# The causal convolution of a recurrence: from VectorE adds to diagonal float32 products on TensorE

## The chip, the core and the metric

The kernel runs on one core of a Trainium2 chip. The metric is the time of one execution in device microseconds (us). TensorE does the matrix products into PSUM (the page writes PE for its matmuls and PEld for its weight loads), VectorE is DVE, ScalarE is ACT, GpSimd is POOL and SyncE is SP. Each engine works through its own list of instructions in order; where one waits, all behind it on that engine wait too.

## What is computed

One step of a hybrid encoder layer for 1024 frames of a new stream and 8 running streams of 16 frames (1152 columns in all). A projection feeds two groups, an RG-LRU recurrence and a sparse attention that keeps for each query the 256 best keys by an index score; an output projection and a feed-forward block follow. What the change touches is the convolution ahead of the recurrence:

```python
def causal_conv(xr, prev, w, b):
    T = xr.shape[1]
    xpad = jnp.concatenate([prev, xr], axis=1)     # prev: the 3 rows before
    y = b
    for j in range(CONV_W):                        # CONV_W = 4
        y = y + xpad[:, j:j + T] * w[j]            # w[j]: one factor per channel
    return y, xpad[:, -(CONV_W - 1):]
...
# rglru: xc -> gates r, i (block-diagonal products, sigmoid) -> a, b -> h_t = a_t * h_(t-1) + b_t
# dsa: vals, sel = top_k(idx_score, 256); attention over sel
```

## The kernel before

The program is written as generators ("streams") that a planner steps through: it keeps an estimate of the time at which each engine is free (`self.busy`, `self.pe`, lines 137 to 180) and lets the stream go on that is due first. So the order of the instructions on each engine comes out of those estimates, and after that a scheduler that works with the same priorities orders them again. Between the two, the order on an engine shifts when the estimated cost of anything shifts.

The stages, as the streams run: normalisation and keys (to about 80 us), index scores (to about 195 us), the recurrence (`lru`, 193 to 383 us by the trace), the query projection (`q_proj`), the first half of the output projection with the rotary embedding of the keys (`out_tile`, `k_rope`), attention (`attn`, `sample_attn`), the second half of the output projection, and the feed-forward block, which fills the time from about 770 us.

Two fillers run beside these stages: `topk` finds, bit by bit, the threshold of the 256th best score for each query. One group (tiles 2 to 4) counts on ACT, the other (tiles 5 to 8) on DVE: each of its 32 passes is four counts over 768, 896, 1024 and 528 columns and two or three very short instructions, first on the upper half of the float (`jk<-key,tk_cand`), then on the lower (`jk<-key,tk_cnt`). After the passes each tile gets its mask (`key<-jk`, `s<-s`, `jk<-key,tk_cnt,jk`). The fillers have a lower priority by 400 steps (`LATER`, line 153), so the planner puts a pass where it believes that DVE has nothing else to do. A pass waits for nothing but the pass before.

The recurrence has 4 chunks of 128 channels, each in a main stream (`lru_main`) and a gate stream (`lru_gate`, which is a projection and a GELU). The main stream goes over the 1152 columns in three thirds of 384. Each third is 24 products of the projection (`proj_T`, names `ps<-h,w`), then `conv(t, px)`: ACT copies the projection with its three columns of history into `xp`, ACT writes tap 3 and the bias into `xc`, and DVE adds taps 0, 1 and 2 (`xc<-xp,prm,xc`). In the last third the 8 running streams need adds of their own, so it has six in place of three. The result is split into a high and a low part (`xh`, ACT and POOL), and six products with the gates' block matrices follow (`ps<-xh,bd`). After all thirds: tanh, exp and sqrt on ACT, products on DVE, three scans on DVE (`tr<-tt,tr,ti`) and the copies of the last state (`tail<-tr`), with which a chunk ends. `xc`, `ti` and `tt` share 8 buffers (`LRU_C`); a chunk takes nine of them, so a chunk's second third waits for the scans of the chunk before. `lock("lru")` lets one main stream through its projection at a time.

`mm4` (line 207) is a product in plain float32; the compiler makes two instructions of each. Before, it is used only for a warm-up and for index scores of the running streams. All other products are of the `float32r` kind with operands split in two, three products for one (`mm3`).

Of the kernel before, what the change touches and what calls it, by code (L numbers as in the profile page):

```python
# [9 lines left out]
F32 = mybir.dt.float32  # L10
# [4 lines left out]
AF = mybir.ActivationFunctionType  # L15
# [15 lines left out]
NB = 8  # L31
# [50 lines left out]
class Kernel:  # L82
# [123 lines left out]

    def mm4(self, out, lhsT, rhs, start, stop):

        self.pe += 4 * rhs.shape[1] / 2400.0
        self.nc.tensor.matmul(out, lhsT, rhs, start=start, stop=stop)  # L210

    def tr(self, out, in_):
# [816 lines left out]
    def lru_main(self, n, c, lp):  # L1029
# [13 lines left out]
        bd = lp.tile([128, 2, 2, 128], F32R, tag="bd", name="bd", bufs=self.BD)  # L1043
        self.hi(bd[:, :, 0, :], braw, "pool")
        self.lo(bd[:, :, 1, :], braw, bd[:, :, 0, :], "pool")
        xps, xhs, xcs, G = [], [], [], []
        trs = []

# [2 lines left out]
                yield 0.3  # L1051
            self.c_free -= k

        def conv(t, px):
            self.begin()
            xc = third("xc")
            xcs.append(xc)
            n = 384 if t < 2 else 256
            xp = lp.tile([128, 411], F32, tag="xp", name="xp", bufs=self.XP)
            if t == 0:  # L1060
                nc.gpsimd.memset(xp[:, 0:3], 0.0)
            else:
                nc.gpsimd.tensor_scalar(xp[:, 0:3], xps[-1][:, 384:387], 1.0, 0.0, op0=ALU.mult, op1=ALU.add)
            S.activation(xp[:, 3:3 + n], px[:, :n], AF.Copy)
            xs = xp[:, 259:411].rearrange("p (b j) -> p b j", b=NB)
            if t == 2:
                S.activation(xs[:, :, 3:19], px[:, 256:384].rearrange("p (b j) -> p b j", b=NB), AF.Copy)
                nc.gpsimd.tensor_scalar(xs[:, :, 0:3], prm[:, c, 16:40].rearrange("p (b j) -> p b j", b=NB), 1.0, 0.0,
                                        op0=ALU.mult, op1=ALU.add)
            xps.append(xp)  # L1070
            S.activation(xc, px[:, :384], AF.Identity, scale=prm[:, c, 3:4], bias=prm[:, c, 4:5])
            for j in range(3):
                wj = prm[:, c, j:j + 1]
                o = xc[:, :n]
                V.scalar_tensor_tensor(o, xp[:, j:j + n], wj, o, op0=ALU.mult, op1=ALU.add)
                if t == 2:
                    o = xc[:, 256:384].rearrange("p (b j) -> p b j", b=NB)
                    V.scalar_tensor_tensor(o, xs[:, :, j:j + 16], wj, o, op0=ALU.mult, op1=ALU.add)
            if t == 2:
                nc.gpsimd.tensor_scalar(tail[:, c, 0:3], xp[:, 256:259], 1.0, 0.0, op0=ALU.mult, op1=ALU.add)  # L1080
                nc.gpsimd.tensor_scalar(tail[:, c, 3:27].rearrange("p (b j) -> p b j", b=NB), xs[:, :, 16:19], 1.0, 0.0,
                                        op0=ALU.mult, op1=ALU.add)
            xh = lp.tile([128, 2, 384], F32R, tag="xh", name="xh", bufs=self.XH)
            self.split(xh, xc, "act", "pool")
            xhs.append(xh)
            return self.end() + self.LRU_LAT
# [16 lines left out]
        for t in range(3):  # L1103
            px = self.ps()
            yield from self.proj_T(px[:, :384], w, self.h[t])
            yield from claim(1)
            ready.append(conv(t, px))
            yield 0.0
            yield from claim(2)
            while not t and not self.tr_free:  # L1110
                yield 0.3
            self.tr_free -= not t
            if t >= self.LAG:
                yield from self.until(ready[t - self.LAG])
                gates(t - self.LAG)
                yield 0.0
# [629 lines left out]
```

## Time and profile before

| | us |
|---|---|
| median of 3 runs | 1593.06 |
| lowest and highest of them | 1591.72, 1593.10 |
| the profiled execution, whole | 1592.46 |
| its span, first to last instruction | 1590.7 |

| engine | busy, us | share of the span |
|---|---|---|
| PE, matmuls | 1449.3 | 91% |
| PEld, weight loads | 1323.5 | 83% |
| DVE | 942.0 | 59% |
| ACT | 595.0 | 37% |
| POOL | 308.1 | 19% |

A busy PE is not PE at its peak: matmuls are pipelined and their ends are modelled, and TensorE's clock is granted in shares of full speed (1.00 is 2.4 GHz). The shares are averages over stages; the rows below tell them apart by stretches of the span.

### The profile page before, as it was taken

Reading aid. Unit: us, or ns where it says so; the run is one execution under the profiler, and the core shown is the slowest. Engines: PE = TensorE matmul, PEld = TensorE weight load, DVE = VectorE, ACT = ScalarE, POOL = GpSimd, SP = SyncE. Lnnn points to the kernel's source line nnn. Section 1 sums busy time; section 2 is a strip of 40 time slices with the busy share of each in tenths; the row PEclk is TensorE's granted clock in tenths of the full one; section 3 lists DMA queues with packets and bytes.
Section 4 is the critical chain, followed back from the end, with each engine's and each line's share of the span. In section 5 each row is a group of like instructions: output and inputs, shape, how many; then the busy total and the mean of one; then the engine's idle time right before and its main releaser. Section 6 shows DMA issues by size and latency. Waiting matters only on the chain.

```text
span 1590.7 us, 20862 instructions
## 1 busy us (share of the span) xinstructions
PE 1449.3 (91%) x7754; PEld 1323.5 (83%) x7754; DVE 942.0 (59%) x2024; ACT 595.0 (37%) x1417; POOL 308.1 (19%) x453
## 2 busy tenths in 40 slices
PE   6889887758856699999999999999999999999998
PEld 6877686758745588878999999999998989898987
DVE  7567899999999888858514242424333342424143
ACT  5458866764402687855411121202020202121100
POOL 4315135553675434500000000000000000000000
PEclk7999898888978799999999999999999999999999
DMA  7201101101400001220302020202020202011102
GB/s 237 54 16 42 34 16 29 29 27 34 152 30 22 1 2 39 66 68 25 96 14 59 22 66 14 76 4 80 0 80 1 80 10 71 27 54 42 38 1 119
DMA packets 93798, 74.65 MB, mean 47 GB/s; under 512 B 13236, under 2 KB 84532, under 8 KB 93696
## 3 DMA queue, kind: packets, MB, share of 16 engines
q1 hardware_dynamic: 93696, 73.32, 15.4%
q8 instruction: 61, 1.00, 0.3%
q14 instruction: 41, 0.34, 0.1%
HBM read 67.03 MB, written 6.27 MB: 46 GB/s over the span
## 4 chain that ended last, share of the span: by engine, by line
PE 67%; DVE 21%; issue 5%; ACT 4%; POOL 2%; DMA 1%; SPq 0%; DVEq 0%; ACTq 0%; POOLq 0%
PE ps L205 63%; DVE jk L66 8%; PE ps L215 3%; DVE xc L66 2%; DVE tk_cand L66 1%; DVE tr L66 1%; ACT jk L66 1%; DVE qn L66 1%; DVE s L66 1%; DVE ti L66 1%; ACT relu L66 1%; DMA x<-in_x_prompt_dram 1%; DVE acc L66 1%; ACT m L66 1%; DVE qeo L66 1%
## 5 line engine op out<-in xcount | busy, mean ns | idle before, releaser
L205 PE MATMUL ps<-hf,w 128*128 128x384 f32 x2556 | 460.5, 338 | 0.0
L205 PEld LDWEIGHTS ps<-hf,w 128*128 128x128 f32 x2556 | 451.4, 187 | 0.8
L205 PE MATMUL ps<-w,a 128*128 128x512 f32 x999 | 239.1, 390 | 0.0
L66 DVE TENSOR_TENSOR acc<-ps,acc 128x512 f32<-128x512 f32 x234 | 161.3, 690 | 119.2 <-PE ps L205 118.7
L205 PEld LDWEIGHTS ps<-w,a 128*128 128x128 f32 x999 | 187.3, 188 | 40.1
L66 DVE TENSOR_TENSOR sg<-ps,sg 128x384 f32<-128x384 f32 x66 | 36.8, 557 | 281.3 <-PE ps L205 280.8
L66 ACT ACTIVATE w<-raw 128x512 fp32r<-128x512 f32 x128 | 77.9, 629 | 300.1 <-PE ps L205 220.9
L66 DVE TENSOR_TENSOR w<-raw,w 128x512 fp32r<-128x512 f32 x116 | 76.8, 687 | 84.6 <-ACT w L66 84.4
L66 ACT ACTIVATE a<-sg 128x384 fp32r<-128x384 f32 x66 | 34.5, 523 | 221.8 <-DVE sg L66 221.8
L205 PE MATMUL ps<-hf,rest 128*128 128x384 f32 x612 | 114.5, 334 | 0.0
L205 PE MATMUL ps<-w,rest 128*128 128x512 f32 x324 | 85.2, 413 | 30.2 <-POOL rest L66 30.1
L205 PE MATMUL ps<-h,w 128*128 128x384 f32 x576 | 108.3, 348 | 0.0
L205 PEld LDWEIGHTS ps<-hf,rest 128*128 128x128 f32 x612 | 106.9, 188 | 0.2
L205 PEld LDWEIGHTS ps<-h,w 128*128 128x128 f32 x576 | 106.3, 197 | 0.0
L205 PEld LDWEIGHTS ps<-w,rest 128*128 128x128 f32 x324 | 62.0, 197 | 46.0 <-POOL rest L66 32.3
L205 PE MATMUL ps<-w,h 128*128 128x256 f32 (+1 forms) x600 | 98.3, 322 | 2.0 <-DVE to L66 2.0
L205 PEld LDWEIGHTS ps<-w,h 128*128 128x128 f32 x600 | 86.4, 197 | 8.3 <-DVE to L66 2.3
L66 ACT ACTIVATE jk<-s,tk_cand 128x384 bf16<-128x384 f32 (+2 forms) x96 | 69.7, 726 | 26.5 <-DVE tk_cand L66 24.1
L66 ACT ACTIVATE sg<-ps 128x384 f32<-128x384 f32 x66 | 32.1, 486 | 122.3 <-PE ps L205 122.3
L66 DVE TENSOR_SCALAR_CACHE_REDUCE jk<-key,tk_cnt 128x768 bf16<-128x768 int16 (+1 forms) x64 | 66.8, 1043 | 1.0
L66 DVE TENSOR_SCALAR_CACHE_REDUCE jk<-key,tk_cand 128x768 bf16<-128x768 bf16 (+1 forms) x64 | 66.7, 1041 | 0.2
L205 PE MATMUL ps<-xh,bd 128*128 128x384 f32 x72 | 22.2, 430 | 45.4 <-ACT xh L66 40.5
(263 smaller groups left out, 2179.4 us busy)
## 6 DMA issues: line engine op xcount, KB each, us to landing
raw<-in_w_ffn_in_dram SPq DMA_DIRECT2D x44, 512.0 KB
raw<-in_w_ffn_out_dram SPq DMA_DIRECT2D x22, 512.0 KB
raw<-in_w_in_dram SPq DMA_DIRECT2D x16, 512.0 KB
out_dram<-acc SPq DMA_DIRECT2D x9, 512.0 KB
x<-in_x_prompt_dram SPq DMA_DIRECT2D x8, 512.0 KB
acc<-in_x_prompt_dram SPq DMA_DIRECT2D x8, 512.0 KB
tab<-in_rope_dram SPq DMA_DIRECT2D x34, 64.0 KB
raw<-in_w_out_dram SPq DMA_DIRECT2D x4, 512.0 KB
```

The costliest lines, as they stand in the source:

```text
L66: return f(*args, **kw)
L205: self.nc.tensor.matmul(out, lhsT, rhs, start=start, stop=stop)
L215: self.nc.tensor.transpose(out, in_, self.ident[0:n, 0:n])
```

## The change

The adds on DVE go. `taps` is a new tile with four diagonal matrices for each chunk, made by four ACT instructions each from the identity (16 in all). `conv` is split in two: `streams(t, px)` makes the shifted input `xp` as before and the main stream now waits for it (by the planner's estimate) before it goes on; the new `conv(t)` multiplies the four shifted views of `xp` by the four diagonal matrices with `mm4`, summed in one PSUM bank (eight such products in the last third, four for 256 columns and four for 128), and ACT then writes `xc` from PSUM with the bias. `mm4`'s estimate counts all columns of a view with more than two dimensions.

```diff
     def mm4(self, out, lhsT, rhs, start, stop):
-        self.pe += 4 * rhs.shape[1] / 2400.0
+        self.pe += 4 * np.prod(rhs.shape[1:]) / 2400.0
...
+        taps = lp.tile([128, 4, 128], F32, tag="taps", name="taps", bufs=2)
+        for j in range(4):
+            S.activation(taps[:, j, :], self.ident, AF.Identity, scale=prm[:, c, j:j + 1])
...
-            S.activation(xc, px[:, :384], AF.Identity, scale=prm[:, c, 3:4], bias=prm[:, c, 4:5])
-            for j in range(3):
-                wj = prm[:, c, j:j + 1]
-                o = xc[:, :n]
-                V.scalar_tensor_tensor(o, xp[:, j:j + n], wj, o, op0=ALU.mult, op1=ALU.add)
-                if t == 2:
-                    o = xc[:, 256:384].rearrange("p (b j) -> p b j", b=NB)
-                    V.scalar_tensor_tensor(o, xs[:, :, j:j + 16], wj, o, op0=ALU.mult, op1=ALU.add)
...
+        def conv(t):
+            xp, n = xps[t], 384 if t < 2 else 256
+            pc = self.ps()
+            for j in range(4):
+                self.mm4(pc[:, :n], taps[:, j, :], xp[:, j:j + n], j == 0, j == 3)
+            if t == 2:
+                xs = xp[:, 259:411].rearrange("p (b j) -> p b j", b=NB)
+                for j in range(4):
+                    self.mm4(pc[:, 256:384].rearrange("p (b j) -> p b j", b=NB), taps[:, j, :], xs[:, :, j:j + 16],
+                             j == 0, j == 3)
+            S.activation(xc, pc[:, :384], AF.Identity, bias=prm[:, c, 4:5])
...
             yield from self.proj_T(px[:, :384], w, self.h[t])
+            yield from self.until(streams(t, px))
             yield from claim(1)
-            ready.append(conv(t, px))
+            ready.append(conv(t))
```

The order on the engines shifts with it. First PE at the first chunk's second third, before (`h` is the input, `w` the projection's weights, `xh,bd` the gates' products, `x12` counts equal rows):

```order
L205 MATMUL ps<-h_0_95,w 128x384 x12
L205 MATMUL ps<-h_1_96,w 128x384 x6
L205 MATMUL ps<-xh,bd 128x384 x2
L205 MATMUL ps<-h_0_99,w 128x384 x4
L205 MATMUL ps<-xh,bd 128x384 x4
L205 MATMUL ps<-h_0_99,w 128x384 x8
L205 MATMUL ps<-h_1_100,w 128x384 x12
L205 MATMUL ps<-xh,bd 128x384 x6
```

And now:

```order
L205 MATMUL ps<-h_0_95,w 128x384 x12
L205 MATMUL ps<-h_1_96,w 128x384 x11
L210 MATMUL ps<-xp,taps 128x384 x4
L205 MATMUL ps<-xh,bd 128x384 x6
L205 MATMUL ps<-h_0_99,w 128x384 x12
L205 MATMUL ps<-h_1_100,w 128x384 x12
L205 MATMUL ps<-h_1_96,w 128x384
L210 MATMUL ps<-xp,taps 128x256 x4
```

The products with `taps` stand between the projection of another stream and the gates' products of the third before.

Then DVE at the end of the last chunk, before (`jk,tk_cnt<-key,tk_cnt` is one count of a pass on the lower half, `tail<-tr` the copies that end the chunk):

```order
L66 SCALAR_TENSOR_TENSOR tr<-tt,ti 128x384
L66 TENSOR_SCALAR jk_911,tk_cnt<-key,tk_cnt 128x1024
L66 SCALAR_TENSOR_TENSOR tr<-tt,tr,ti 128x384
L66 TENSOR_SCALAR jk_911,tk_cnt<-key,tk_cnt 128x528
L66 SCALAR_TENSOR_TENSOR tr<-tt,tr,ti 128x384
L66 TENSOR_SCALAR tk_cand<-tk_cnt 128x4
L66 COPY tail<-tr 128x1
L66 COPY tail<-tr 128x8
L66 SCALAR_TENSOR_TENSOR tk_cnt<-tk_cand,tk_cnt 128x4
L66 TENSOR_SCALAR jk_911,tk_cnt<-key,tk_cnt 128x768
```

And now (`s_891` is the score of tile 5 and `s_890` that of tile 4, `key<-jk` the scan of a mask):

```order
L66 SCALAR_TENSOR_TENSOR tr<-tt,ti 128x384
L66 TENSOR_SCALAR jk_911<-s_891,tk_cnt 128x768
L66 SCALAR_TENSOR_TENSOR tr<-tt,tr,ti 128x384
L66 SCALAR_TENSOR_TENSOR key<-jk_911 128x768
L66 TENSOR_SCALAR s_891,tk_cnt<-s_891,tk_cnt 128x768
L66 TENSOR_SCALAR jk_912<-s_890,tk_cnt 128x640
L66 SCALAR_TENSOR_TENSOR tr<-tt,tr,ti 128x384
L66 TENSOR_SCALAR tk_cnt<-tk_cnt 128x1
L66 TENSOR_SCALAR s_890,tk_cnt<-s_890,tk_cnt 128x640
L66 COPY tail<-tr 128x1
L66 COPY tail<-tr 128x8
```

Before, 3 of the 16 passes on the lower half stand ahead of this place; now all 16 do, and the masks have begun.

Last, DVE at the first sums of the output projection (`acc<-ps,acc`), before:

```order
L66 TENSOR_SCALAR jk_911,tk_cnt<-key,tk_cnt 128x1024
L66 TENSOR_TENSOR qn<-qn,rp 128x256
L66 TENSOR_TENSOR tail<-tail 128x72
L66 TENSOR_TENSOR acc<-ps,acc 128x512
L66 TENSOR_TENSOR kn<-kn,tab 128x128
L66 TENSOR_TENSOR acc<-ps,acc 128x512
L66 TENSOR_SCALAR tk_cnt<-tk_cnt 128x1
L66 TENSOR_TENSOR qn<-qn,rp 128x256
L66 TENSOR_SCALAR jk_911,tk_cnt<-key,tk_cnt 128x528
```

And now (`qn` is the queries' rotary embedding, `kn` the keys'):

```order
L66 TENSOR_TENSOR kn<-kn,rp 128x128
L66 TENSOR_TENSOR acc<-ps,acc 128x512
L66 TENSOR_TENSOR qn<-qn,tab 128x256
L66 TENSOR_TENSOR acc<-ps,acc 128x512
L66 TENSOR_TENSOR qn<-qn,rp 128x256
L66 CAST jk_911<-s_894 128x528
L66 TENSOR_TENSOR qn<-qn,tab 128x256
L66 TENSOR_TENSOR qn<-qn,rp 128x256
```

Between the sums there are no counts left; the cast belongs to the sample attention's preparation, which runs when all masks are done.

## Rows read from the trace of the kernel before

**Rows 1.** The page: sums by engine, and three strips of 40 slices.

```profile
PE 1449.3 (91%) x7754; PEld 1323.5 (83%) x7754; DVE 942.0 (59%) x2024; ACT 595.0 (37%) x1417; POOL 308.1 (19%) x453
...
PE   6889887758856699999999999999999999999998
...
DVE  7567899999999888858514242424333342424143
...
PEclk7999898888978799999999999999999999999999
```

**Rows 2.** Stretches of the span: from:to, length, busy us, granted clock, DMA.

```profile
core 0: us, PE busy (x) PEld busy (x) DVE busy (x) ACT busy (x) POOL busy (x), PEclk, DMA share, GB/s
193.00:383.00 190.00, 142.30 (x783) 137.72 (x781) 187.28 (x470) 121.87 (x235) 81.46 (x111) 0.87 0.09 24
383.00:446.00 63.00, 50.15 (x334) 46.65 (x335) 62.28 (x137) 28.06 (x176) 39.73 (x64) 0.86 0.40 132
446.00:527.00 81.00, 49.55 (x195) 38.43 (x193) 79.15 (x158) 16.01 (x45) 46.28 (x61) 0.79 0.05 14
527.00:560.00 33.00, 26.40 (x132) 20.37 (x133) 29.02 (x108) 27.07 (x78) 19.21 (x31) 0.83 0.01 1
560.00:1590.00 1030.00, 1019.63 (x5501) 944.48 (x5499) 450.21 (x873) 277.71 (x569) 56.87 (x68) 1.00 0.15 45
```

**Rows 3.** Who waited for whom, 200 to 380: us in total, times, longest.

```profile
PE ps L205 <- ACT xh L66: 40.5, 8, 13.7
...
ACT xh L66 <- DVE xc L66: 11.9, 5, 3.9
```

**Rows 4.** Groups by form, 195 to 375: count | busy us, mean ns | idle before.

```profile
L66 DVE SCALAR_TENSOR_TENSOR xc<-xp,prm,xc 128x384 f32<-128x384 f32 x24 | 16.3, 681 | 0.0
...
L66 DVE SCALAR_TENSOR_TENSOR xc<-xp,prm,xc 128x256 f32<-128x256 f32 x12 | 8.1, 673 | 0.0
...
L66 DVE SCALAR_TENSOR_TENSOR xc<-xp,prm,xc 128x128 f32<-128x128 f32 x12 | 5.6, 464 | 0.0
...
L66 ACT ACTIVATE xp<-ps 128x128 f32<-128x128 f32 x4 | 1.1, 277 | 0.0
```

**Rows 5.** DVE in order of time: start us, us, what.

```profile
343.52 0.61 DVE L66 SCALAR_TENSOR_TENSOR xc<-xp,prm,xc 128x384 f32<-128x384 f32 x1
344.05 0.16 DVE L66 TENSOR_TENSOR ti<-ti,s 128x8 f32<-128x8 f32 x1
```

**Rows 6.** Float32 products of line 210: instruction groups, and six in order of time.

```profile
L210 PE MATMUL ps<-yF x32: 383/386/647, 122.3 to 185.4; 128*128 128x264 f32 x32
...
122.29 1.50 PE L210 MATMUL ps<-yF 128*128 128x264 f32 x6
```

**Rows 7.** Counts of the top-k on DVE, 380 to 440, as groups.

```profile
L66 DVE TENSOR_SCALAR_CACHE_REDUCE jk<-key,tk_cnt 128x528 bf16<-128x528 int16 (+3 forms) x35 | 36.3, 1037 | 0.6
```

**Rows 8.** DVE's three marks: last chunk's end, first sum, first attention score.

```profile
382.61 1.06 DVE L66 COPY tail<-tr 128x1 f32<-128x1 f32 x2
...
445.59 0.67 DVE L66 TENSOR_TENSOR acc<-ps,acc 128x512 f32<-128x512 f32 x1
...
526.67 0.29 DVE L66 CUSTOM_DVE_ANT_0 m<-ps,kn 128x128 f32<-128x128 f32 x1
```

**Rows 9.** 446 to 527: DVE and POOL work on tiles jk, and on tiles s.

```profile
446.00:527.00 81.00, 0.00 (x0) 32.56 (x48) 0.00 (x0) 6.18 (x4) 0.79 0.05 14
...
446.00:527.00 81.00, 7.63 (x12) 0.00 (x0) 9.64 (x8) 0.79 0.05 14
```

**Rows 10.** Who waited for whom, 440 to 500.

```profile
PE ps L205 <- POOL rest L66: 30.1, 5, 10.2
...
POOL kn L66 <- DVE kn L66: 11.3, 4, 5.6
```

**Rows 11.** PE in order of time: query projection and the first output tiles.

```profile
358.61 4.26 PE L205 MATMUL ps<-w,h 128*128 128x256 f32 x19
...
420.59 2.92 PE L205 MATMUL ps<-w,rest 128*128 128x512 f32 x12
...
426.12 2.93 PE L205 MATMUL ps<-w,rest 128*128 128x512 f32 x12
```

More of the change, by code (lines that the diff above doesn't have):

```diff
@@ L1052, in claim, with streams @@
             self.c_free -= k
-        def conv(t, px):
+        def streams(t, px):
             self.begin()
-            xc = third("xc")
-            xcs.append(xc)
             n = 384 if t < 2 else 256
@@ L1064, in conv @@
             S.activation(xp[:, 3:3 + n], px[:, :n], AF.Copy)
-            xs = xp[:, 259:411].rearrange("p (b j) -> p b j", b=NB)
             if t == 2:
+                xs = xp[:, 259:411].rearrange("p (b j) -> p b j", b=NB)
                 S.activation(xs[:, :, 3:19], px[:, 256:384].rearrange("p (b j) -> p b j", b=NB), AF.Copy)
@@ L1069, in conv @@
                                         op0=ALU.mult, op1=ALU.add)
-            xps.append(xp)
-            S.activation(xc, px[:, :384], AF.Identity, scale=prm[:, c, 3:4], bias=prm[:, c, 4:5])
-            for j in range(3):
-                wj = prm[:, c, j:j + 1]
-                o = xc[:, :n]
-                V.scalar_tensor_tensor(o, xp[:, j:j + n], wj, o, op0=ALU.mult, op1=ALU.add)
-                if t == 2:
-                    o = xc[:, 256:384].rearrange("p (b j) -> p b j", b=NB)
-                    V.scalar_tensor_tensor(o, xs[:, :, j:j + 16], wj, o, op0=ALU.mult, op1=ALU.add)
-            if t == 2:
                 nc.gpsimd.tensor_scalar(tail[:, c, 0:3], xp[:, 256:259], 1.0, 0.0, op0=ALU.mult, op1=ALU.add)
@@ L1082, in conv @@
                                         op0=ALU.mult, op1=ALU.add)
+            xps.append(xp)
+            return self.end()
+        def conv(t):
+            self.begin()
+            xp, n = xps[t], 384 if t < 2 else 256
[3 more added lines that the diff above has]
+            if t == 2:
+                xs = xp[:, 259:411].rearrange("p (b j) -> p b j", b=NB)
+                for j in range(4):
+                    self.mm4(pc[:, 256:384].rearrange("p (b j) -> p b j", b=NB), taps[:, j, :], xs[:, :, j:j + 16],
+                             j == 0, j == 3)
+            xc = third("xc")
+            xcs.append(xc)
+            S.activation(xc, pc[:, :384], AF.Identity, bias=prm[:, c, 4:5])
             xh = lp.tile([128, 2, 384], F32R, tag="xh", name="xh", bufs=self.XH)
```

## The prediction

> **What bounds the kernel now.** The first view is the page with its sums and strips [rows 1]. By the sums TensorE is the engine to spare: 1449.3 us of matmuls, 91% of the span, against 59% on DVE. The strips say that this is an average over two regimes. From about slice 21 PE is full and its clock granted in full; in slices 5 to 13 it is DVE that is full, and PE falls to 5 to 8 tenths at 0.7 to 0.9 of the clock.
>
> The second view, busy time by stretches, puts numbers to it [rows 2]. In the recurrence DVE is busy for 187.3 of 190 us, in the query projection for 62.3 of 63, in the output projection for 79.2 of 81: 328.7 of 334 us, 98%. PE has 142.3 of 190, 50.2 of 63 and 49.6 of 81. Only from 560 us on is PE the bound, with 1019.6 of 1030 us at clock 1.00. So the stretch from 193 to about 527 us lasts as long as DVE's list, and what comes after is a block of TensorE work that slides as a whole: a microsecond won at the first attention score, DVE's mark at 526.67 [rows 8], is one at the end.
>
> The third view, who waited for whom, agrees: in the recurrence PE waits 40.5 us for `xh`, and ACT waits for DVE's `xc` before it can write `xh` [rows 3].
>
> By the Trainium skill, Perfetto Trace Analysis, § Identifying the Most-Contended Engine, the engine with the highest occupancy is to be improved first, and for Tensor that occupancy is read as the busy share of its weight loads. Over the whole span that share is 83% against DVE's 59%; taken alone, the rule would have this change load the bound engine. Its neighbour section on optimization strategy allows that the contended engine changes over time, which is what [rows 2] show. What the first reading gives is a rival below.
>
> **Removed from DVE.** 24 adds of 384 columns, 12 of 256 and 12 of 128: 16.3 + 8.1 + 5.6 = 30.0 us busy [rows 4]. Instructions of DVE overlap a little: an add begins at 343.52 and lasts 0.61, and the next instruction begins at 344.05, 0.08 before its end [rows 5]. 48 x 0.08 = 4 us, so **26 us** of DVE's list go. Their bound from below is 24 (a step of 0.5 each), from above 30.
>
> **Added to TensorE.** Twelve thirds with four products of 384 columns (in the last thirds eight, of 256 and 128, together the same). Each is two instructions. The same line's float32 products in the trace: six instructions of 264 columns end 1.50 us after the first begins, the last being 0.386 long; five steps in 1.11 us, 0.222 each, 0.84 ns a column [rows 6]. So 384 columns take 0.32 us, and 12 x 4 x 2 x 0.32 = **31 us of PE**. Upper bound: 0.386 us each with no overlap for 264 columns, 0.56 for 384, 54 us. Both fit into the recurrence: 142.3 + 31 = 173 of 190 us [rows 2]; with 54 it would be 196, just over. I take 31, since the products with `taps` come in runs of eight as those of the row do in runs of six, and 142.3 is busy time that includes waiting for a slower clock.
>
> **Added elsewhere.** ACT writes 16 matrices at 0.28 us each [rows 4], 4.5 us, on an engine with 121.9 busy of 190 [rows 2]: nothing on the path. ACT's own `xc` stays, only its source is another PSUM bank. The chain of a third becomes ACT `xp`, PE 4 x 2 x 0.32 = 2.6 us, ACT `xc`, ACT `xh`; before, three adds at 0.53 to 0.68 with counts queued between them. About the same length, and DVE no longer in it. What hides it is the counts: they wait for nothing of this, so while there are passes left DVE has work whenever the chain is late. Without that cover the cost would be up to 2.6 us a third, 31 us.
>
> **Moved.** The planner sees DVE with more room and puts filler there: ahead of the last `tail<-tr`, at 382.6 [rows 8], stand now 13 more passes. 52 counts at 1.04 less the overlap, 1.00 [rows 7], 52 us; some 31 very short instructions at the 0.16 us of [rows 5], 5; eleven of the masks at 0.6 to 1 us [rows 9], 9; less 26. So DVE's list up to the end of the recurrence is **40 us longer**, and the recurrence would end near 423. This by itself is neither gain nor loss, since the filler had to be done anyway. It matters for what waits for the recurrence.
>
> The first sum of the output projection stands at 445.6 [rows 8]. Ahead of it now lies nearly all of the top-k work of the stretch 446 to 527: 48 instructions on `jk`, 32.6 us, those on `s`, 7.6 less some 3 that count in both [rows 9], a cast, and some 20 short ones, 3: 40 to 45. Nine adds of the queries' embedding, 5 us, go the other way. 42 - 5 - 26 makes +11, with the cast about +14: first sum near **460**. Ahead of the first score, at 526.7, the order has only six more mask instructions and three fewer others: -26 + 2 = -24, so **503** if DVE never waits.
>
> **What is late next.** Here lies the catch. The stage from first sum to first score was 81 us because DVE was full of counts. Without them DVE needs 79 - 42 + 5 = 42 us there. POOL needs 46.3 - 9.6 = 37 (its work on `s` is masks, gone ahead) [rows 2, 9]. PE needs seven output tiles of 5.53 us, the step between the first two [rows 11], 39. Three engines of 37 to 42 us wait for each other in turn: PE for POOL's `rest`, 30.1 us, POOL for DVE's `kn`, 11.3 [rows 10]. Those waits are long partly because DVE and POOL were then held up by masks and counts, and there is no cover left for them. The stage can't be under 42; if half of PE's 30 and all of the 11 stay in series with the shorter engines it is 39 + 15 + 11 = 65. I take 48 to 50, nearer the lower end, because the longest waits stood behind work that has left the stage. PE's own way there fits: its query projection begins at 358.6 [rows 11], in the gap behind the last chunk; 40 us more filler delays the scans that free the shared buffers, so I put that at about 385, and with 62 us to the first output tile (420.6 - 358.6), shorter where DVE was in its way, it comes near 447 to 457, just ahead of the first sum. First score then at 460 + 50 = **510**, 17 us earlier than 526.7.
>
> **The sum.** Profiled execution 1592.5 (span 1590.7 and 1.8 around it), less 17, 1575.5; the median of the runs is 0.6 above the profiled one: 1576, and I write **1575**.
>
> **The rivals.**
> First, the full gain: the output stage hides its chain and DVE's list stays the bound to the end of the stretch. 1592.5 - 26 = 1566 (1562 with the larger bound of the adds). For it: DVE was 98% busy in three stages with different chains [rows 2]. Against: 41 us of counts kept it so, and they stand earlier now.
> Second, the gain is eaten: the stage takes 61 to 68 us, the upper end above. 1589 to 1596, within what can be told from no change.
> Third, slower: the output stage was never as long as DVE's list but as its chain (POOL `kn` after DVE `kn`, `rest` after POOL, PE after `rest` [rows 10]) and keeps all its 81 us behind a first sum that comes 14 to 16 later. 1592.5 + 16 = 1608. It decides from the point where the stage shrinks by less than those 14 to 16 of 81. For it: PE's 30 us of waiting; against: DVE busy 79 of 81, and 40 of that leaves.
> Fourth, TensorE is the bound everywhere, as the whole span's shares have it [rows 1]: +31, 1623. Against: PE has 48 us to spare in the recurrence [rows 2]. The Trainium skill's rule named above, read on the whole span, is this rival.
> Fifth, DVE isn't relieved where it matters, because the planner returns all of it to filler and the recurrence ends 40 us later: that is what the order shows, and it is already in the sum; its harm would be the second or the third.
>
> **How the numbers follow.** Forecast (1568 to 1588): 0.55. Full gain (1560 to 1567): 0.17. Eaten: 0.13. Slower by the chain (1597 to 1610): 0.11. TensorE: 0.04. 0.2%, 3.2 us, is about what a measurement of this kernel tells from no change. Faster 0.55 + 0.17 = 0.72; same 0.13; slower 0.15. The range takes in the first three and leaves out the last two: 1560 to 1598.
>
> **What the profile after would show.** No `xc<-xp` on DVE; 128 instructions `ps<-xp,taps` on PE (4 x (4 + 4 + 8) x 2), 31 us in steps of 0.32 for 384 columns, else that term was wrong. DVE at 98% or more from 193 to about 420, the last tail copy near 423, the first sum near 460, the first score near 510, and the first idle time of DVE between those two, ended by POOL or PE. PE's wait for `xh` well under 40 us. If DVE idles for more than 5 us in the recurrence, the cover failed; if the stage from first sum to first score is above 65 us, the chain was the bound and the forecast is wrong; below 45, the full gain has it.

## The result

| | us |
|---|---|
| before, median | 1593.08 |
| after, median of 4 runs | 1607.45 |
| lowest and highest of them | 1604.22, 1608.10 |
| ratio after to before, 95% interval | 1.0087, 1.0070 to 1.0105 |
| the profiled execution of after, and its span | 1607.94, 1606.2 |

The changed kernel is slower by 14.4 us; 1575 was forecast, with a range of 1560 to 1598. The page of after, sums and the same three strips as in [rows 1]:

```profile
PE 1477.5 (92%) x7882; PEld 1341.0 (83%) x7882; DVE 929.6 (58%) x1976; ACT 593.4 (37%) x1430; POOL 307.9 (19%) x453
...
PE   6889878787487899999999999999999999999998
...
DVE  7557899999978788858624252424243333424243
...
PEclk9999999898698999999999999999999999999999
```

DVE lost 12.4 us of busy time where the adds were 30.0, and PE has a hole in slice 11 (about 402 to 442 us) that was not there. The same stretches as in [rows 2], cut at after's own marks (end of the recurrence, first sum, first score, 33 us more, the rest):

```profile
core 0: us, PE busy (x) PEld busy (x) DVE busy (x) ACT busy (x) POOL busy (x), PEclk, DMA share, GB/s
193.00:429.00 236.00, 176.45 (x931) 161.25 (x929) 229.51 (x569) 122.79 (x252) 81.22 (x115) 0.87 0.07 20
429.00:485.00 56.00, 46.47 (x310) 42.13 (x311) 44.88 (x65) 26.89 (x175) 52.44 (x60) 0.87 0.46 145
485.00:545.00 60.00, 47.83 (x200) 37.51 (x198) 45.09 (x86) 15.04 (x44) 40.39 (x65) 0.91 0.07 21
545.00:578.00 33.00, 29.09 (x159) 23.71 (x158) 28.96 (x112) 31.21 (x86) 14.54 (x29) 0.90 0.01 1
578.00:1606.00 1028.00, 1017.73 (x5484) 941.95 (x5482) 448.13 (x867) 274.57 (x562) 55.19 (x65) 1.00 0.15 45
```

The recurrence now takes 236 us instead of 190. The two stages behind it take 116 instead of 144, and there DVE idles for 26 of 116 us, where before it was busy for all but 2.6 of 144 [rows 2]. The marks of [rows 8], after, in order of time on DVE:

```profile
429.24 0.34 DVE L66 COPY tail<-tr 128x1 f32<-128x1 f32 x2
...
484.80 0.68 DVE L66 TENSOR_TENSOR acc<-ps,acc 128x512 f32<-128x512 f32 x1
...
545.13 0.29 DVE L66 CUSTOM_DVE_ANT_0 m<-ps,kn 128x128 f32<-128x128 f32 x1
...
722.63 0.68 DVE L66 TENSOR_TENSOR acc<-ps,acc 128x512 f32<-128x512 f32 x1
```

Against before, the recurrence ends 46.6 us later, the first sum comes 39.2 later, the first score 18.5. The last row is the first sum of the output projection's second half, and before it stands here:

```profile
706.97 0.68 DVE L66 TENSOR_TENSOR acc<-ps,acc 128x512 f32<-128x512 f32 x1
```

From this mark to the end of the span it is 883.7 us before and 883.5 after, and between 883.5 and 884.4 in every kernel of this study. So the whole question lies between 193 us and this mark.

**Where the 39 us at the first sum are from.** ScalarE (ACT) at the end of the last chunk, after, in order of time, with its wait in brackets:

```profile
392.49 1.35 ACT L66 ACTIVATE tr<-tr,m 128x1152 f32<-128x1152 f32 x1
415.43 1.28 ACT L66 ACT_TABLE_LOAD   x1 [21.59 <-DVE tr L66]
416.72 1.16 ACT L66 ACTIVATE tr<-tr 128x1152 f32<-128x1152 f32 x1
429.69 0.38 ACT L66 ACTIVATE qn<-ps 128x256 f32<-128x256 f32 x1 [11.81 <-DVE tail L66]
```

The exp (`tr<-tr,m`) is done at 393.8. The sqrt behind it needs DVE's `tr`, and its table load waits 21.6 us for it; before, and in gate11 below, where some of the filler is held back, the same wait is 5.8 and 3.3 us. Before:

```profile
372.57 1.28 ACT L66 ACT_TABLE_LOAD   x1 [5.84 <-DVE tr L66]
...
383.79 0.39 ACT L66 ACTIVATE qn<-ps 128x256 f32<-128x256 f32 x1 [8.75 <-DVE tk_cnt L66]
```

In gate11:

```profile
377.35 1.28 ACT L66 ACT_TABLE_LOAD   x1 [3.32 <-DVE tr L66]
...
388.60 0.39 ACT L66 ACTIVATE qn<-ps 128x256 f32<-128x256 f32 x1 [8.79 <-DVE tk_cand L66]
```

In after's 21.6 us DVE is not idle:

```profile
404.06 0.76 DVE L66 TENSOR_SCALAR_CACHE_REDUCE jk<-key,tk_cnt 128x528 bf16<-128x528 int16 x1
...
408.26 1.26 DVE L66 TENSOR_SCALAR_CACHE_REDUCE jk<-key,tk_cnt 128x1024 bf16<-128x1024 int16 x1
...
409.91 0.61 DVE L66 SCALAR_TENSOR_TENSOR jk<-ps,tk_cnt,jk 128x384 bf16<-128x384 f32 x1
...
411.12 2.05 DVE L66 SCALAR_TENSOR_TENSOR tt<-tr,tt 128x384 f32<-128x384 f32 x3
...
414.03 1.32 DVE L66 SCALAR_TENSOR_TENSOR tr<-tt 128x384 f32<-128x384 f32 x2
```

It counts: of the 17.3 us from 393.84 to 411.12 it is busy for 16.7, with 13.6 of them on `key`. The step `tt<-tr,tt`, whose inputs ACT had written by 393.8, starts at 411.12, behind passes that have that place in the list. From the end of the exp to the last tail copy it is 15.9 us before, 35.4 after and 13.9 in gate11.

The copies of the query projection out of PSUM (`qn<-ps`) wait for the tail copy itself. The first of them begins 0.1 us after the last tail copy ends, in after (429.58 and 429.69), before (383.67 and 383.79) and gate11 (388.49 and 388.60) alike, and so in every kernel of this study but hurry, where POOL's last read of a tile of the recurrence, `yF<-yF,tr`, comes 0.9 us later still and ends the wait. The program has a reason that fits all of them: the pool of `qn` is opened where the pool of the recurrence's tiles has been closed (lines 323 to 332), so that `qn` takes over their memory and has to wait until they have been read for the last time. Until then PE can run the projection ahead only as far as the eight PSUM banks (line 268) reach. It began at 384.62, had six tiles of 24 products by 404.0, and stood still for 24.0 us from there to the first output tile, against 5.0 us before and 5.8 in gate11:

```profile
384.62 4.47 PE L205 MATMUL ps<-w,h 128*128 128x256 f32 x24
...
389.68 14.29 PE L205 MATMUL ps<-w,h 128*128 128x256 f32 x120
410.58 0.82 PE L215 MATMUL ps<-ident,tail 128*36 128x128 f32 x3 [6.62 <-DVE jk L66]
420.20 4.43 PE L205 MATMUL ps<-w,h 128*128 128x256 f32 x24 [8.79 <-DVE jk L66]
429.63 0.40 PE L215 MATMUL ps<-ident,tail 128*36 128x128 f32 x1 [5.00 <-DVE tail L66]
433.60 32.81 PE L205 MATMUL ps<-w,h 128*128 128x256 f32 x264 [3.57 <-ACT sq L66]
466.25 2.91 PE L205 MATMUL ps<-w,rest 128*128 128x512 f32 x12
```

Its waits of 6.62 and 8.79 us end when a mask on DVE has read a bank (`jk<-ps,tk_cnt,jk`, to 410.52 above, and again to 420.14): the masks of tiles 2 to 4, which the order has moved ahead, use PSUM too, and so take two of the eight banks. In before and in gate11 their first scan stands behind the tail copy. The last two waits end with the tail copy and with ACT's copies behind it.

The rows for the same place before are [rows 11]: 62.0 us from the projection's begin to the first output tile, now 81.6, in gate11 60.4. From the last tail copy to the first output tile it is 37.9 us before and 36.9 after, and between 34 and 41 in every kernel here. So an end of the recurrence that comes 46.6 us later puts the first output tile off by nearly as much (45.7). The stages behind it win 30 of these back: the mark of the second half comes 15.7 us later.

### The profile page after: what moved, and what is told of

Its sections match the earlier page's. It is cut to its first block, busy times and chain, and to the rows that moved or that the text cites. A ratio compares the mean times of both kernels' runs of the same rounds, so it can differ in the third digit from the quotient of the medians.

```text
span 1606.2 us, 21084 instructions
## 1 busy us (share of the span) xinstructions
PE 1477.5 (92%) x7882; PEld 1341.0 (83%) x7882; DVE 929.6 (58%) x1976; ACT 593.4 (37%) x1430; POOL 307.9 (19%) x453
## 4 chain that ended last, share of the span: by engine, by line
PE 69%; DVE 16%; ACT 6%; POOL 4%; issue 4%; DMA 1%; SPq 0%; POOLq 0%; ACTq 0%; DVEq 0%
PE ps L205 65%; DVE jk L66 8%; PE ps L215 3%; DVE tr L66 1%; ACT jk L66 1%; DVE tk_cand L66 1%; POOL rp L66 1%; DVE s L66 1%; DVE ti L66 1%; ACT relu L66 1%; ACT m L66 1%; PE ps L210 1%; ACT qeo L66 1%; ACT yF L66 1%; POOL w L66 1%
## 5 line engine op out<-in xcount | busy, mean ns | idle before, releaser
L205 PE MATMUL ps<-w,h 128*128 128x256 f32 (+1 forms) x600 | 98.4, 323 | 12.4 <-DVE jk L66 8.8
L205 PEld LDWEIGHTS ps<-w,rest 128*128 128x128 f32 x324 | 61.8, 195 | 24.7 <-POOL rest L66 10.9
L210 PE MATMUL ps<-xp,taps 128*128 128x384 f32 (+2 forms) x128 | 39.7, 461 | 30.2 <-ACT xp L66 28.5
```

## The experiments

Two theories stood at first. **Order**: the filler that the planner and the scheduler put ahead of the recurrence's end does the harm. **Products**: the 31 us on PE do it, wherever the filler stands. The tool for both is a tiny DVE instruction (four columns) beside a pass's counts that reads a value of a chunk's `tr` and multiplies it by zero; the passes behind it can't be scheduled ahead of the instruction that wrote the value. In the gates this is the chunk's sqrt, which is written over the exp (the expectations call it the exp output); up to one pass still stands between it and the tail copies. "Counts ahead" are the instructions `jk,tk_cnt<-key` that stand in DVE's list ahead of the last `tail<-tr`, of 128 in all. Differences to the kernel before are to its runs on the same chip.

| kernel | counts ahead | last tail | first score | DVE idle, 193 to last tail | time, us | ratio, 95% interval |
|---|---|---|---|---|---|---|
| before | 76 | 382.7 | 526.7 | 2.7 | 1593.1 | |
| after | 128 | 429.3 | 545.1 | 6.5 | 1607.5 | 1.0070 to 1.0105 |
| hurry | 128 | 441.1 | 553.8 | 5.8 | 1615.4 | 1.0128 to 1.0158 |
| gate7 | 100 | 405.4 | 533.8 | 25.8 | 1594.9 | 1.0004 to 1.0023 |
| gate11 | 84 | 388.0 | 525.8 | 28.0 | 1588.9 | 0.9966 to 0.9985 |
| gate11_again | 84 | 388.8 | 526.9 | 27.2 | 1588.8 | 0.9972 to 0.9990 |
| gate13 | 76 | 388.2 | 526.3 | 29.2 | 1592.1 | 0.9984 to 1.0003 |
| noadds | 92 | 376.2 | 519.5 | 5.2 | 1579.0 | 0.9899 to 0.9929 |
| waits_alone | 92 | 383.9 | 515.4 | 5.7 | 1579.3 | 0.9897 to 0.9926 |
| gates_a | 94 | 404.5 | 542.1 | 24.7 | 1603.9 | 1.0054 to 1.0084 |
| gates_b | 102 | 402.3 | 537.7 | 18.1 | 1600.1 | 1.0031 to 1.0065 |
| no_dependency | 94 | 396.5 | 533.8 | 21.9 | 1598.8 | 1.0027 to 1.0051 |
| products_only | 74 | 391.8 | 535.6 | 16.3 | 1599.8 | 1.0022 to 1.0052 |
| one_tap | 104 | 393.2 | 523.9 | 4.1 | 1585.0 | 0.9936 to 0.9966 |
| short_chain | 94 | 391.6 | 530.3 | 11.3 | 1593.7 | 0.9998 to 1.0017 |
| before_held | 64 | 377.9 | 523.8 | 12.7 | 1600.7 | 1.0032 to 1.0062 |
| hybrid | 84 | 397.6 | 535.0 | 23.8 | 1599.1 | 1.0032 to 1.0063 |

### The order alone: hurry, gate7, gate11

**hurry**: the kernel before, with the order of after.

```diff
+        while self.pass_b > self.HURRY[c]:      # HURRY = (99, 13, 7, 0)
+            yield 0.3
         S.activation(trs[0], trs[0], AF.Exp, scale=m4[:, c:c + 1], bias=m4[:, c:c + 1])
+        if c:
+            x = trs[0][:, 0:4]
+            V.scalar_tensor_tensor(x, self.pass_t, 0.0, x, op0=ALU.mult, op1=ALU.add)
```

> The kernel before, with its adds on DVE and without products, but chunks 2, 3 and 4 may not begin their exp before 3, 9 and 16 lower-half passes stand ahead (a tiny DVE instruction reads the threshold of the pass): counts ahead of the chunks' tail copies 40, 83, 107, 128 instead of 40, 58, 64, 76; the changed kernel has 58, 76, 101, 128. The total work of DVE is the same. Theory 1: last tail at 382.6 + 52 = 435, and from there 116 us to the first score as in the changed kernel, 551 instead of 526.7: about 1615 us. Theory 2 or a view that filler is free wherever it stands: 1593.

1615.4, +22.9 us, the recurrence's end at 441.1 and 112.7 us from there to the first score. No work was changed but for three instructions of four columns: DVE did the same passes earlier, and then had 7 idle us between the recurrence's end and the first sum and 12 behind it. So filler ahead of the recurrence's end is not free. The order is not quite that of after: the second chunk has 83 counts ahead of its end where after has 76, and the recurrence ends 11.8 us later than there. The 22.9 us are the price of this order, not a part of after's 14.4.

**gate7, gate11**: the changed kernel, with one wait, ahead of lower-half pass 9 or 5.

```diff
+                if b == self.HOLD:              # 7 or 11
+                    while self.last_tr is None:
+                        yield 0.3
+                    nc.vector.scalar_tensor_tensor(t, self.last_tr, 0.0, t, op0=ALU.mult, op1=ALU.add)
                 yield from self.topk_count(g, t, True)
```

> The changed kernel with one more tiny DVE instruction: the lower-half pass number 9 (of 16) reads a value of the last chunk's exp output, so the seven passes from there and all masks can't stand ahead of it. Counts ahead of the last tail copy: 100 instead of 128 (76 before). Theory 1 (the harm is the filler that was pulled ahead of the recurrence's end; it holds back ScalarE's exp/sqrt chain and behind it the query projection, and leaves DVE nothing to do later): last tail copy at 382.6 + 24 - 26 = 381 instead of 429, DVE idle under 10 us between there and the first attention score, first score 505 to 515, 1570 to 1580 us. Theory 2 (the 31 us of float32 products on TensorE are the price, wherever the filler stands): the recurrence ends after 410 and the time stays above 1597.

> As the run before, but the wait stands at the fifth lower-half pass: 84 counts ahead of the last tail copy. Theory 1: DVE's own list would end the recurrence at 382.6 + 8 - 26 = 365; if the chain of ScalarE and TensorE allows that, DVE stays full and the first score again comes at 505 to 515, 1570 to 1580 us; if not, DVE idles in the recurrence for the difference, and the time is by so much worse than that of the wait at pass 9. Theory 2: above 1597.

1594.9 and 1588.9, +2.4 and -3.6: against after's +14.4 the order of a few passes is worth 12 and 18 us of the changed kernel, so its 1607 is not the price of the products alone. But neither came to 1570 to 1580, and DVE idled for 26 and 28 us inside the recurrence, which the first theory had only as a possibility for gate11. What bounds gate11 there is seen in the last chunks, up to the last product with the gates' matrices (`ps<-xh,bd`, done at 370.0) and from there to the recurrence's end, beside the whole recurrence:

```profile
193.00:388.00 195.00, 168.40 (x913) 155.28 (x911) 167.00 (x439) 120.80 (x248) 76.77 (x111) 0.93 0.09 24
330.00:370.00 40.00, 39.46 (x224) 36.26 (x223) 22.16 (x49) 19.68 (x33) 27.12 (x35) 1.00 0.14 40
370.00:388.00 18.00, 15.90 (x136) 15.68 (x134) 12.09 (x25) 6.45 (x7) 4.78 (x8) 1.00 0.01 2
```

From 330 to 370 us PE is busy for 39.5 of 40 us at a granted clock of 1.00, all but 3.5 of it on products of the recurrence, and DVE for 22. With little filler in the way PE sets when the last chunk's products are done. The 18 us behind them are the chain through ACT and DVE, as before (18.6, from 364.1); PE is busy there too, but with the query projection, which does not end the recurrence.

### What the removal is worth: noadds, waits_alone

**noadds** is the kernel before without the loop over taps 0 to 2:

```diff
-            for j in range(3):
...
-                V.scalar_tensor_tensor(o, xp[:, j:j + n], wj, o, op0=ALU.mult, op1=ALU.add)
...
-                    V.scalar_tensor_tensor(o, xs[:, :, j:j + 16], wj, o, op0=ALU.mult, op1=ALU.add)
```

> The kernel before with taps 0 to 2 left out: 48 adds on DVE gone, no products on TensorE, nothing else edited (the output lacks these taps). 92 counts ahead of the last tail copy, 16 more than before. What the removal is worth at most. Theory 1: tail at 382.6 + 16 - 26 = 373, DVE's list shorter by 26 at the first score, 1567 to 1575 us. Theory 2: the same, since no products are there. Theory 3 (what DVE is relieved of is lost to waits anyway, whatever the order): 1585 or more.

1579.0, 13.5 us less than before, between the forecasts of the first and the third theory: half of the 26. From 193 us to the mark of the second half the time in which DVE runs anything (covered time) fell from 470.9 to 448.4, 22.5, and its idle time grew from 43.0 to 51.0, 8. **waits_alone** adds the four waits of gates_a to it:

> The run without adds and without products (taps 0 to 2 left out of the output), now with the four waits of the run with waits a. Counts ahead of the tail copies 44, 64, 76, 92, as without the waits; so it shows what the waits themselves cost. If they are free: tail 376 to 379, 1577 to 1582 us, and the difference to waits a, some 25 us, is the price of the products. If they cost 5 to 10 us of DVE's idle time: tail 382 to 386, 1584 to 1590, and the products cost 14 to 20.

1579.3: the tail comes 7.7 us later and the first sum 8.7, the time is the same. The waits are free here, and neither mark is a measure of the time by itself.

### What the products cost: gates_a, gates_b, no_dependency, products_only

**gates_a** is the changed kernel with counts ahead as in noadds, by four waits:

```diff
+    HOLD = {10: 0, 15: 1, 18: 2, 22: 3}         # pass: chunk
...
+        self.nc.vector.scalar_tensor_tensor(cnt, self.last_tr[c], 0.0, cnt, op0=ALU.mult, op1=ALU.add)
```

> The changed kernel with four tiny DVE instructions that make passes 11, 16, 19 and 23 of 32 read a value of the exp output of chunks 1, 2, 3 and 4. Counts ahead of the chunks' tail copies: 46, 64, 76, 94, almost as without the adds (44, 64, 76, 92; 1579 us) and with the changed kernel's 58, 76, 101, 128 undone. So against the run without adds this shows the price of the products alone, and against the changed kernel that of the order alone. Theory 1 (products fit beside DVE, 31 us of PE into 48 us of room): last tail 376 to 380, 1579 to 1585 us. Rival (with the filler spread as before, TensorE is the recurrence's bound, as in the wait at pass 5, where it was busy 55 of 58 us in the last two chunks): DVE idles some 10 to 25 us in the recurrence, tail near 385 to 390, 1587 to 1593.

> As the run before with the waits one to two passes later (passes 12, 17, 21 and 25): 50, 68, 86, 102 counts ahead of the tail copies, eight more at the end, 8 us of DVE. Where DVE's list ends the recurrence, tail and time come up to 8 us later than there, less what DVE idled; where TensorE ends it, the time is the same and DVE's idle time shorter.

1603.9, 24.6 us over waits_alone with the same waits and nearly the same counts, and worse than the rival's 1587 to 1593. gates_b, eight counts more, ends the recurrence at 402.3 instead of 404.5 with 7 us less idle time on DVE, and is 3.9 us faster, which neither branch of its expectation had: it was not DVE's list that ended it. In **no_dependency** the products multiply the diagonal matrices by themselves, so nothing waits for anything new:

```diff
-                self.mm4(pc[:, :n], taps[:, j, :], xp[:, j:j + n], j == 0, j == 3)
+                self.mm4(pc[:, :384], taps[:, j, :], taps[:, 0:3, :], j == 0, j == 3)
...
-            S.activation(xc, pc[:, :384], AF.Identity, bias=prm[:, c, 4:5])
+            S.activation(xc, px[:, :384], AF.Identity, scale=prm[:, c, 3:4], bias=prm[:, c, 4:5])
```

> The run with waits a, with all products, but on constant operands (the diagonal matrices by themselves), so that TensorE waits for nothing and nobody waits for them; xc is written as in the run without adds (taps 0 to 2 left out of the output). Counts ahead of the tail copies 46, 64, 76, 94. Theory C (what is paid is TensorE's time itself, because its idle time in the recurrence is no room but part of the chain): tail and time as with waits a, 400 or later, about 1600. Theory D (TensorE has room, only the dependency costs): tail at 376 to 382, 1579 to 1585.

1598.8: 19.5 of the 24.6 us are there although nothing waits for the products. The place where they come in is PE's chain: its last product with the gates' matrices is done at 355.2 in waits_alone, at 369.7 here and at 382.8 in gates_a. What else no_dependency keeps of the change, a PSUM bank for each third, the 16 matrices on ACT and the wait for `xp` in the planner's order, was not taken away by itself. **products_only** puts the same constant products into the kernel before, adds kept:

> The kernel before, its adds on DVE kept, with the twelve sets of four float32 products (31 us of TensorE) put in on constant operands, whose result nobody reads, and waits that hold the filler where it was: counts ahead of the tail copies 46, 58, 62, 74 (before: 40, 58, 64, 76). My step that 31 us fit into TensorE's 48 idle us of the recurrence: tail at 383 to 386, 1593 to 1596 us. Theory C (that idle time is no room: TensorE waits there for a chain that goes through it, and each us of products lengthens it): tail 395 to 405, DVE idle 12 us or more there, 1603 to 1612.

1599.8, +6.4 us: between the two forecasts. The recurrence, 193 to 392 us:

```profile
193.00:392.00 199.00, 173.55 (x878) 155.70 (x877) 182.65 (x471) 129.45 (x256) 80.03 (x111) 0.93 0.08 23
```

PE went from 142.3 [rows 2] to 173.6 us busy: that is the 31. The stage grew by 9 all the same, with PE's idle time down from 47 to 25 and DVE's up from 3 to 16. So some two thirds of the products went into PE's idle time, and the rest made the stage longer. That PE's remaining idle time is waiting for a chain that runs through it fits, but is not shown by itself; and the waits that hold the filler may have a price of their own here, as they have in before_held below.

### Length or hop: one_tap, short_chain, hybrid

**one_tap** keeps one of the four products (`range(1)`), without waits; **short_chain** the same with the waits of gates_a.

> The changed kernel with one of the four products for each third (the output lacks taps 1 to 3; TensorE has 8 us of them instead of 31), no waits added: the scheduler itself then puts 52, 64, 84, 104 counts ahead of the tail copies. Theory: what pulls filler ahead is how long the scheduler holds the products, and the time follows the counts: near the run with waits b, 1583 to 1592, well below 1607.

> The run with waits a, with one product for each third in place of four (taps 1 to 3 left out of the output): the same counts ahead of the tail copies (46, 64, 76, 94), the same place in the chain (TensorE waits for xp, ScalarE for TensorE), 8 us of products instead of 31. There the last tail came at 404.5, and at 376.2 without products. Theory A (the length of the products sits on the recurrence's chain): tail at 376 + 28 x 8 / 31 = 383, 1583 to 1587 us. Theory B (it is the extra hop, TensorE's in-order list waiting for ScalarE's xp, whatever the products' length): tail near 400, about 1600 us.

one_tap: 1585.0, as expected, 22 us below after. With a quarter of the products the scheduler pulled 28 counts ahead of the place they had before, instead of 52, and DVE stayed filled (4.1 us idle). short_chain: 1593.7, between the two theories. Its work is that of one_tap; the waits, free without products, cost some 8 us here. So their length is a part of the products' price, and not in proportion: 8 us of them with their hop cost 14 over waits_alone, 31 cost 25. And a price found with the waits holds for the order that the waits make: without them the same 8 us cost 6 (one_tap over noadds).

**hybrid** is gate11 with tap 0 back on DVE, 8 us less on PE:

```diff
-            for j in range(4):
...
+            for j in range(1, 4):
...
+            V.scalar_tensor_tensor(o, xp[:, 0:n], prm[:, c, 0:1], o, op0=ALU.mult, op1=ALU.add)
...
```

> The changed kernel with the wait at pass 5 (run gate11: 1588.9 us, DVE idle 28 us in the recurrence, TensorE idle only 24), and tap 0 given back to DVE: three products for each third, then one add. TensorE has 8 us less, DVE 9 us more, which its idle time there should take. If TensorE's time is what ends the recurrence, tail near 382 and 1582 to 1586 us. If the add in the chain (ScalarE xc, DVE add, ScalarE xh) waits behind counts again: 1589 to 1596.

1599.1, 10 us worse than gate11 and above both forecasts. The waits in its recurrence, us in total, times, longest:

```profile
PE ps L205 <- ACT xh L66: 21.0, 4, 6.5
...
ACT xh L66 <- DVE xc L66: 15.6, 6, 8.8
```

These are the two of [rows 3], which the change had all but taken away (PE's wait for `xh` is 4.8 us in gate11). One DVE step in the chain brings them back, behind whatever DVE has in its list. So gate11 is not only bound by the length of PE's work; that the chain no longer passes through DVE also lets PE run through. The counts differ a little (54 and 68 ahead of the first two chunks' ends, in gate11 58 and 76).

### From the other side: before_held, gate13, gate11_again

**before_held** is the kernel before with waits at two passes (`HOLD = {13: 1, 14: 2}`), 12 counts fewer ahead.

> The kernel before with two waits of the kind used above (passes 14 and 15 read the exp of chunks 2 and 3): 40, 57, 62, 64 counts ahead of the tail copies instead of 40, 58, 64, 76. Its adds stay on DVE. If the filler in the last chunk costs about its own time, as the run with more filler ahead had it (+52 counts, +58 us of tail, +22 us of time), 12 counts fewer bring the tail 8 to 12 us earlier and the time down by 3 to 6, to 1587 to 1590. If DVE's list is the bound from 193 to 527 us as I read it in the prediction, the time can't fall: 1593 or a little more.

1600.7, +7.4, above both forecasts, though the recurrence ends 4.8 us earlier and the first score comes 2.8 earlier. The last mask's count on DVE moved from 533.5 to 553.0, and the masks are read by the attention: the mark of the second half comes 7.0 later (714.0). That the late masks put it off is read from the order; no run moved them alone. It would mean that the filler has a due time on both sides. This also corrects a step of the prediction: the first score is not yet the place from which all slides as a block.

> As the run with the wait at pass 5 of the lower half, two passes earlier: 58, 72, 72, 76 counts ahead of the tail copies, in sum the 76 of the kernel before. Best version so far if the trend of the waits at passes 9 and 5 goes on (1594.9, 1588.9): 1584 to 1588, tail near 382. If DVE's idle time now costs as much as the earlier tail brings: 1588 to 1592.

> The kernel of run gate11 once more, with more rounds: the interval there was 0.9966 to 0.9985 of the kernel before. If that holds: 1587 to 1590 us beside 1592 to 1594.

gate13 gives 1592.1, not told apart from before, where the trend forecast 1584 to 1588: fewer counts ahead than in gate11 gain nothing. gate11_again gives 1588.8, ratio 0.9981 (0.9972 to 0.9990): the one order in which the change is a gain, by 3 us, shown twice.

## Why the prediction was wrong

**Where the error lies.** The first score was put at 510 and came at 545.1, 35 us later. 6 of them were there at the recurrence's end (423 forecast, 429.3 measured), 19 more were added on the way to the first sum (37 us forecast, 55.5 measured), and 10 in the stage behind it (50 and 60.3).

**The bound** was half right. DVE is busy for 98% of 193 to 527 us, but a good part of it is filler that is put wherever DVE would idle, so a full DVE doesn't show that its list sets the end. Taking 26 us off the list gave 13.5 (noadds). The Trainium skill, Perfetto Trace Analysis, § Identifying the Most-Contended Engine, calls occupancy "a fair measure of how close you are to roofline" for Vector. It does not say what a microsecond off that engine is worth, and here it was worth half. (PE is full from slice 15 of the strips on, not from "about slice 21"; [rows 2] have it right, at 560 us.)

**Removed, 26 us**: the size held. Covered time fell by 22.5 in noadds. The step from there to the time didn't.

**Added, 31 us**: the size held where PE did not wait ahead of the products: PE's busy time went from 142.3 to 173.6 in products_only, and eight instructions of 384 columns take 2.74 us there, in steps of 0.32. In after the rows of `ps<-xp,taps` come to 39.7. Three of the sets stand right behind a wait of 8 to 10 us for `xp`, and these took longer: the eight at 365.14, behind 9.96 us of waiting, took 4.52 us at a granted clock of 0.62, the eight at 342.90 took 2.74 at 1.00.

The first step that failed is "both fit into the recurrence: 142.3 + 31 = 173 of 190". Busy time of two engines that wait for each other can't be laid side by side like that. The same products cost 6.4 us where DVE still had its adds, and 19.5 in the order of waits a, where it hadn't. That DVE's list and PE's chain were nearly equal bounds, and what was taken from one uncovered the other, fits both, but the two runs also differ in their order (74 and 94 counts ahead), so it is not shown. The wait for `xp`, which the prediction called as long as the old chain, is another 5 (gates_a over no_dependency). Its trace in after, who waited for whom from 195 to 429 us:

```profile
PE ps L210 <- ACT xp L66: 28.5, 4, 10.0
```

Before, PE waited 40.5 us for `xh` [rows 3], in after 6.9; the wait moved from one step of the chain to another. DVE idled for 6.5 us in the recurrence, more than the 5 that the prediction named as the sign that the cover failed.

**Moved.** The recurrence's end was put at 423 and came at 429.3. That this "by itself is neither gain nor loss" is the second step that failed, and by the marks the larger one in after itself (19 of the 35 us). The prediction let the query projection run beside the late end: begun at 385, with the 62 us of before, it would bring the first output tile at 447 and the first sum at 460, 37 us behind the recurrence's end. The begin was right (384.6). But the projection's copies can't start ahead of the last tail copy, so it ran until its PSUM banks were full and stood: 81.6 us in place of 62, the first output tile 36.9 us behind the tail copy, the first sum at 484.8, 55.5 behind it. Before, that distance was 62.9, and no kernel here has it under 55. Holding the filler back in gate11 brings the tail to 388.0, the projection to 60.4 us and the time to 1588.9; the reverse, filler pulled ahead in the kernel before, costs 22.9 us (hurry). I had listed what DVE's queue gains, and not who waits for the place in it that now comes late.

**What is late next**: the stage from first sum to first score took 60.3 us, not 48 to 50. It stayed under the 65 that would have meant the chain. One of its three terms was too small from the start: PE was given 39 us, where [rows 2] have it busy for 49.6 in that stretch, and after it is 47.8 of 60.

**The rivals.** The third one's 1608 is the time that was measured, and its mechanism is not what happened: it needed a stage that keeps its 81 us behind a first sum 14 to 16 later; the stage lost 21 and the first sum came 39 later. The fifth named the right place, the recurrence's end, and was priced at nothing. The fourth, PE as the bound, has some of it: with the filler held as in waits a, 20 of its 31 us are there. The second one's time does not follow from its stage: behind a first sum at 460, 61 to 68 us give 1587 to 1594, not 1589 to 1596; it changes nothing here.

**The sum as the runs give it**, each against the kernel before on its own chip: adds away -14.1 (waits_alone), products without dependency +19.7, the wait for `xp` +5.4, and the filler where the scheduler puts it by itself instead of waits a +3.3. That this comes to the measured 14.4 proves nothing, since each part is the difference of two neighbouring runs. Another way through the runs gives other parts: adds away -13.5 (noadds), products with the wait of gate11 +9.9, its wait taken out +18.0. So both products and order cost, and how the price is shared between them depends on the order in which the other is looked at.

**What stays open.** That the place of the filler is worth 18 us (gate11 against after, one and the same work but for a four-column instruction) is shown, but not why gate11 beats gates_a by 15: it has 58 and 76 counts ahead of the first two chunks' ends where gates_a has 46 and 64, and 4 each in the last two chunks where gates_a has 12 and 18. It would fit that filler costs little in the first chunks and much in the last, behind which the query projection stands; no run changed the one without the other. And what in the scheduler's prices for the float32 products pulls the passes ahead was not looked into; one_tap shows only that fewer products pull fewer. Nor was `qn` tried in memory of its own, which would show what the wait for the tail copy costs by itself.

## What to carry to other kernels

An engine that is kept full by filler is not shown to be the bound by its busy share: take the filler out of the sum, follow the chain through all engines, and count another engine's idle time as room only if it doesn't wait there for the same chain. When a change makes a scheduler move work, price the move by itself, and look for everything that waits for the instruction that now comes late: here it was the next stage, whose tiles take over the memory of this one. The cheap test for all of it is a false dependency on a tiny operand, which holds the filler in place while the work is changed. Run it without the change too: it was free in waits_alone, and cost some 8 us in short_chain.

## What the runs showed that was not expected

The same 18 adds of the queries' embedding took very different times. Before (383 to 527 us), least, median and greatest ns:

```profile
L66 DVE TENSOR_TENSOR qn<-qn,tab x18: 408/486/1528, 391.6 to 469.9; 128x256 f32<-128x256 f32 x18
```

After (429 to 545 us):

```profile
L66 DVE TENSOR_TENSOR qn<-qn,tab x18: 523/1079/1526, 439.5 to 506.4; 128x256 f32<-128x256 f32 x18
```

In gate11 (388 to 526 us):

```profile
L66 DVE TENSOR_TENSOR qn<-qn,tab x18: 408/420/1112, 396.5 to 473.8; 128x256 f32<-128x256 f32 x18
```

With the adds of `rp` this is about 11 us more DVE time in after than before, and one reason why DVE's busy time fell by only 12.4. In after most of these adds fall into a stretch where POOL is busy for 52.4 of 56 us, before into one with 39.7 of 63 [rows 2]. Add by add it shows too: of the 72 adds of `tab` and `rp` in before and gate11, the 22 during which POOL ran nothing took 408 to 424 ns each, and all 24 that took over 450 ran beside POOL for about half their time or more. In after none ran without POOL. Others beside POOL were as short as the 22, so which of POOL's instructions matter stays open. The Trainium skill, Perfetto Trace Analysis, § Optimizing Scalar/DVE Operations, says that GpSimd and DVE share a read port of SBUF; the rows agree with that, but no run here changed it by itself.
